# Key products made once and kept masked in DRAM, and a new order of the feature tiles in a two-layer streaming trunk

## The chip, the cores and the metric

The kernel runs on one core of one Trainium2 chip. The metric is device time in microseconds (us) of one execution; the median of the runs is compared. One more execution was taken with the hardware profiler, and all views below are of that one.

## The reference

Two layers are applied to 1024 prompt tokens and to 8 samples of 16 tokens, which share the weights. Each layer projects the normed input once and feeds four branches; the change touches the first, a recurrent mix with a matrix state for each of 4 heads:

```python
z = rms_norm(x, p['norm_g']) @ p['w_in']
...
prev = jnp.concatenate([shift_prev[:, None, :], za[:, :-1]], axis=1)
zs = za + p['rw_mu'] * (prev - za)          # receptance r, key k, value v, two low-rank inputs
...
def step(s, inp):
    r_t, w_t, k_t, v_t, kk_t, a_t = inp
    sa = jnp.einsum('bhij,bhj->bhi', s, -kk_t)
    s = (s * w_t[:, :, None, :] + sa[:, :, :, None] * (kk_t * a_t)[:, :, None, :]
         + v_t[:, :, :, None] * k_t[:, :, None, :])
    return s, jnp.einsum('bhij,bhj->bhi', s, r_t)
...
s_t, ys = lax.scan(step, s0, xs)
y = layer_norm(ys) ; out = y + sum(r * k * rk) * v
...
out = x + (concat(A, B, C, D) * silu(gates)) @ p['w_out']
```

The other branches are latent attention, a gated unit over 128 positions, and a pooling of trailing means.

## The kernel before

All 1152 tokens are columns, in three groups g of G = 384. The input projection is done by feature tiles of 128 rows: 24 in each layer, in the order F_ORDER (line 35), each as 3 groups of 24 matmuls of 128x384 into a PSUM tile `pj` (two buffers), because operands and weights are split into a high and a low part. `project` (line 245) runs a list of tiles. `load_weights` (line 229) fetches a tile's weights in four pieces on SP's queue, two tiles ahead; ACT makes the high part `wh`, POOL the low part `wl`. After each group a sink reads `pj`: for keys, receptances and values it is `shift_sink` (line 376), ACT and DVE together.

All other work is written as Python generators in lanes. At the matmul numbers in `ticks`, and at the end of each group, `tick()` advances each lane by one step; `inproj` (line 360) sets how many ticks a tile has (two, three or four in a group: 6, 9 or 12 in a tile). Lane "a" carries the recurrent branch, in this order: `a_elem` (line 427) makes the key operands `KB` and `AR` of one group; `systems` (line 506) makes for each 64-token chunk (16 of the prompt, then 16 and 17 of the samples) four products of keys with keys, masks them on DVE into `ns`, and ACT's queue stores them in `nd` or `nds` in DRAM; after 4 idle steps `solve` (line 520) loads the diagonal blocks and inverts them row by row with two DVE operations for each row: 15 rows for the samples (32 partitions), then 31 rows for the prompt (128 partitions), and stores the results in `dd` and `dds`. `recurrence` (line 707) then takes the chunks one after another, the samples first, three steps each: `prepare` (line 560) of the next chunk loads the solved blocks `tt` and makes `Gm`, the masked products of keys with keys and receptances, again with PE and DVE; `advance` (line 639) moves the state. `groupnorm` (line 722) follows for each group in lane "n".

The order of feature tiles is WDAD and K0 together, K1, R0, R1, V0, V1, D0, GD0, D1, GD1, VC0, VC1, U0, GC0, U1, GC1 (lines 910 to 929), then seven more for attention and gates. `systems` starts in K1, `solve` in V0; `recurrence` is queued after D0, so that its 56 steps run in GD0 to U0. Instructions are put on their engines by a scheduler that follows the written order as a priority but may issue an instruction earlier when its inputs are ready; each engine then works in that order. `Gm`, `tt` and `ns` have two buffers each, the tag "m" for large tiles has eight, PSUM tiles `b` four.

## Time and profile before

| | us |
|---|---|
| median of 3 runs | 1447.55 (1444.83 to 1448.42) |
| the profiled execution | 1447.32, of it a span of 1445.5 |
| PE busy | 1358.6 |
| DVE, ACT, POOL busy | 786.8, 746.6, 465.2 |
| tiles K1 to GC1, first layer | 326.17, of it PE busy 305.41 |
| tiles K1 to GC1, second layer | 319.88, of it PE busy 302.88 |

PE = TensorE's matmuls, PEld its weight loads, DVE = VectorE, ACT = ScalarE, POOL = GpSimd, SP = SyncE, which issues loads. A q behind an engine's name marks its sequencer: an issue of a transfer or a wait. Busy is the time in which an engine has at least one instruction in work; a wait is listed with the instruction that ended it.

### The profile page before, as it was taken

The page shows a single profiled execution, that of the slowest core. Times are in us where ns is not written, and L with a number is a line of the kernel's source. Part 1 is how long each engine was busy: PE and PEld are TensorE (multiplying, and loading weights), DVE is VectorE, ACT ScalarE, POOL GpSimd, SP SyncE. Part 2 cuts the span into 40 slices and gives each one's busy share as a digit, 9 for nine tenths or more (in the row PEclk, how much of TensorE's full clock was granted, in tenths as well). Part 3 has the DMA queues.
Part 4 walks back from the last instruction along what each step waited for, and adds up shares of the span by engine and source line. Part 5 has one row for each costly group of instructions (what it writes and reads, how often), then busy time and mean ns, then how long its engine had stood idle before and what let it go on. Part 6 is the DMA issues. An engine that isn't in the chain of part 4 may idle for free. (4 is left out here: it accounts for less than half of the span.)

```text
span 1445.5 us, 26910 instructions
## 1 busy us (share of the span) xinstructions
PE 1358.6 (94%) x9962; PEld 1160.2 (80%) x9962; DVE 786.8 (54%) x1766; ACT 746.6 (52%) x2013; POOL 465.2 (32%) x600
## 2 busy tenths in 40 slices
PE   4899989999999999999989998999999999899999
PEld 3768868888988886679977788788789788766998
DVE  6984954435235567742287948444532374777211
ACT  6762234655466677642257621555654676866210
POOL 4514404336411033332162234232653111322320
PEclk9799999999999999999999999999999999999999
DMA  7113241110312214033300122321022111131232
GB/s 222 52 32 75 63 102 42 61 49 25 96 46 70 60 37 128 5 116 93 99 22 30 49 64 66 92 69 49 29 71 74 52 57 59 45 103 45 74 95 77
DMA packets 116596, 97.40 MB, mean 67 GB/s; under 512 B 46129, under 2 KB 111345, under 8 KB 116465
## 3 DMA queue, kind: packets, MB, share of 16 engines
q1 hardware_dynamic: 76776, 73.74, 17.6%
q10 hardware_dynamic: 39688, 21.94, 5.1%
q8 instruction: 79, 1.29, 0.4%
q14 instruction: 53, 0.43, 0.1%
HBM read 71.48 MB, written 24.16 MB: 66 GB/s over the span
## 5 line engine op out<-in xcount | busy, mean ns | idle before, releaser
L76 PE MATMUL pj<-xh,wh 128*128 128x384 f32 x1152 | 415.4, 361 | 18.9 <-ACT xh L280 7.2
L76 PE MATMUL pj<-xl,wh 128*128 128x384 f32 x1152 | 396.4, 344 | 2.4 <-POOL xl L282 2.0
L76 PE MATMUL pj<-xh,wl 128*128 128x384 f32 x1152 | 396.3, 344 | 0.0
L242 POOL TENSOR_TENSOR wl<-wr,wh 128x256 fp32r<-128x256 f32 x200 | 157.0, 793 | 465.9 <-ACT wh L241 390.5
L76 PEld LDWEIGHTS pj<-xh,wh 128*128 128x128 f32 x1152 | 221.6, 193 | 41.7 <-ACT sho L400 11.3
L76 PEld LDWEIGHTS pj<-xl,wh 128*128 128x128 f32 x1152 | 222.1, 193 | 9.0 <-POOL xl L282 3.3
L76 PEld LDWEIGHTS pj<-xh,wl 128*128 128x128 f32 x1152 | 221.4, 192 | 6.0 <-issue 4.8
L76 PE MATMUL pj<-yh,wh 128*128 128x384 f32 x384 | 129.3, 337 | 2.4 <-DVE x L1426 2.4
L76 PE MATMUL pj<-yh,wl 128*128 128x384 f32 x384 | 128.6, 335 | 0.0
L76 PE MATMUL pj<-yl,wh 128*128 128x384 f32 x384 | 128.3, 334 | 0.0
L241 ACT ACTIVATE wh<-wr 128x256 fp32r<-128x256 f32 x200 | 81.0, 414 | 84.7 <-PE pj L76 41.0
L242 POOL TENSOR_TENSOR wl<-m,wh 128x256 fp32r<-128x256 f32 x56 | 43.7, 790 | 102.0 <-ACT wh L241 84.4
L76 PEld LDWEIGHTS pj<-yh,wh 128*128 128x128 f32 x384 | 72.1, 188 | 3.7 <-DVE x L1426 2.8
L76 PEld LDWEIGHTS pj<-yl,wh 128*128 128x128 f32 x384 | 72.1, 188 | 0.1
L76 PEld LDWEIGHTS pj<-yh,wl 128*128 128x128 f32 x384 | 72.1, 188 | 0.1
L1293 ACT ACTIVATE X<-b,ng 128x512 f32<-128x512 f32 (+3 forms) x96 | 55.0, 577 | 25.3 <-DVE ng L1285 21.4
L76 PE MATMUL b<-sp,cr 128*128 128x384 f32 (+3 forms) x192 | 59.5, 385 | 3.2 <-POOL sp L99 2.8
L1281 DVE TENSOR_REDUCE mx<-b 128x1 f32<-128x512 f32 (+3 forms) x96 | 53.0, 556 | 9.8 <-PE b L76 8.0
L1422 DVE TENSOR_TENSOR pt<-pj,pt 128x384 f32<-128x384 f32 x24 | 13.4, 557 | 80.6 <-PE pj L76 80.6
L76 PEld LDWEIGHTS st<-X,X 128*64 128x64 f32 x576 | 35.1, 136 | 27.4 <-ACT X L1311 7.6
L241 ACT ACTIVATE wh<-m 128x256 fp32r<-128x256 f32 x56 | 22.4, 413 | 61.0 <-PE pj L76 59.9
L1304 PE MATMUL pj<-cm,X 128*128 128x128 f32 x288 | 48.0, 286 | 5.0 <-ACT X L1293 5.0
(307 smaller groups left out, 2591.7 us busy)
## 6 DMA issues: line engine op xcount, KB each, us to landing
wr<-in_win_dram SPq DMA_DIRECT2D x176, 128.0 KB
m<-in_wout_dram SPq DMA_DIRECT2D x12, 512.0 KB
x<-in_xT_dram SPq DMA_DIRECT2D x12, 384.0 KB
ysp<-m ACTq DMA_DIRECT2D x24, 192.0 KB
pt<-in_xT_dram SPq DMA_DIRECT2D x24, 192.0 KB
ea<-ysp SPq DMA_DIRECT2D x24, 192.0 KB
x1d<-x ACTq DMA_DIRECT2D x24, 192.0 KB
pt<-x1d SPq DMA_DIRECT2D x24, 192.0 KB
```

The lines of the kernel that those rows point to most:

```text
L76: return PE.matmul(out, lhsT=lhsT, rhs=rhs, start=start, stop=stop, skip_group_check=True)
L241: A.activation(out=h, in_=r, func=AF.Copy)
L242: Po.tensor_tensor(out=lo, in0=r, in1=h.bitcast(F32), op=ALU.subtract)
L1281: V.tensor_reduce(out=mx[:, b:b + 1], in_=pc[:, :w], axis=AX.X, op=ALU.max)
L1293: A.activation(out=P[:, :w], in_=pc[:, :w], func=AF.Exp, scale=SCALE, bias=ng, accum_out=sums[pr][:, b, s, h:h + 1])
L1304: PE.transpose(ptp[:, j * 128:(j + 1) * 128], Pb[slot][:, j * 128:(j + 1) * 128], ident)
L1422: V.tensor_tensor(out=xr, in0=ps, in1=xr, op=ALU.add)
```

## The change

- `systems` makes the full products of `Gm` for each chunk (keys with keys and receptances, two groups of PE products and two masks on DVE), stores the two halves of the key part in `nd` or `nds`, and stores the whole of `Gm` in a new DRAM tile `gd`; all three on SP's queue. The separate 64x64 products and `ns` are gone. It takes one step for each chunk instead of one for two.
- `prepare` loads `Gm` from `gd` instead of making it.
- Because `Gm` needs the receptances, `systems(g)` is queued by the sink of R1. The tile order becomes WDAD and K0, V0, R0, K1, R1, V1, D0, GD0, D1, and so on. `solve` follows directly; the idle steps are gone.
- `recurrence` is queued after D1 instead of D0; the tiles from GD1 to GC1 have 12 ticks each (U0 had them before, the others 9).
- The 30 operations of the sample solve go to POOL, issued in one step, with their own scratch `TMs`; the prompt's stay on DVE.

```diff
@@ -32,7 +32,7 @@
 (WDAD, K0, R0, V0, K1, R1, V1, D0, GD0, D1, GD1, VC0, VC1, U0, GC0, U1, GC1,
  GB0, GB1, Q0, Q1K, CK, GA0, GA1) = range(NF)
 
-F_ORDER = (WDAD, K0, K1, R0, R1, V0, V1, D0, GD0, D1, GD1, VC0, VC1, U0, GC0, U1, GC1,
+F_ORDER = (WDAD, K0, V0, R0, K1, R1, V1, D0, GD0, D1, GD1, VC0, VC1, U0, GC0, U1, GC1,
            Q0, Q1K, CK, GB0, GB1, GA0, GA1)
 
 
@@ -359,10 +359,9 @@
 
         def inproj(f, sink):
             ticks = (3,)
-            if f in (K1, R0, R1, V0, V1, D0, GD0, D1, GD1, VC0, VC1, GC0, U1, GC1,
-                     GA0, GA1):
+            if f in (K1, R0, R1, V0, V1, D0, GD0, D1, GA0, GA1):
                 ticks = (2, 5)
-            elif f in (U0, GB0, GB1):
+            elif f in (GD1, VC0, VC1, U0, GC0, U1, GC1, GB0, GB1):
                 ticks = (1, 3, 5)
             project([(l, f)], xh, xl, [sink], ticks)
 
@@ -490,6 +489,8 @@
             def after(g, zs):
                 ex = AR[i][g][:, :, 1, :]
                 Po.tensor_tensor(out=ex, in0=chv(zs), in1=ex, op=ALU.mult)
+                if i == 1:
+                    go("a", systems(g))
             shifted(fr, lambda g: s_tile("gn", 3), after)
 
         def values(fv):
@@ -498,7 +499,9 @@
             vfm.append(v)
 
 
+
         nd, nds = halves(f"nd{l}", 32, 64), halves(f"nds{l}", 4, 64)
+        gd = dr.tile([18, 128, 512], F32, tag=f"gd{l}", name=nm("gd"))
 
         def hp(h):
             return slice(64 * (h % 2), 64 * (h % 2) + 64)
@@ -506,46 +509,53 @@
         def systems(g):
             for cl in range(6):
                 c = 6 * g + cl
-                pn = pb()[:, 0:128].rearrange("p (i t) -> p i t", i=2)
-                for h in range(4):
-                    mm(pn[hp(h), h // 2, :], KB[h // 2][g][hp(h), cl, h % 2, :], AR[h // 2][g][hp(h), cl, 0, :])
-                ns = chp.tile([128, 2, 64], F32, tag="u0", name=nm("ns"), bufs=2)
-                mk = cm[:, C_MP if c < 16 else C_MS, 0:64]
-                V.tensor_tensor(out=ns, in0=pn, in1=mk.unsqueeze(1).broadcast_to([128, 2, 64]), op=ALU.mult)
-                A.dma_start(out=whole(nd, c, 64) if c < 16 else whole(nds, c - 16, 64),
-                            in_=ns.rearrange("p i t -> p (i t)"))
-                if cl % 2:
-                    yield
+                samp = c >= 16
+                Gm = chp.tile([128, 2, 2, 128], F32, tag="gm", name=nm("gm"), bufs=2)
+                mk = cm[:, C_MS if samp else C_MP, :]
+                for hh in range(2):
+                    pg = pb()[:, 0:256].rearrange("p (i t) -> p i t", i=2)
+                    pr = slice(64 * hh, 64 * hh + 64)
+                    for i in range(2):
+                        mm(pg[:, i, :], KB[i][g][pr, cl].rearrange("p a t -> p (a t)"),
+                           AR[i][g][pr, cl].rearrange("p a t -> p (a t)"))
+                    V.tensor_tensor(out=Gm[:, hh], in0=pg, in1=mk.unsqueeze(1).broadcast_to([128, 2, 128]),
+                                    op=ALU.mult)
+                for hh in range(2):
+                    half = nds[2 * (c - 16) + hh] if samp else nd[2 * c + hh]
+                    SY.dma_start(out=half[0:128 * 64].rearrange("(s i t) -> s i t", s=64, i=2),
+                                 in_=Gm[64 * hh:64 * hh + 64, hh, :, 0:64])
+                SY.dma_start(out=gd[c], in_=Gm.rearrange("p h i t -> p (h i t)"))
+                yield
 
         def solve():
             NT = m_tile(1024).rearrange("p (s t) -> p s t", s=32)
             DT = m_tile(1024).rearrange("p (s t) -> p s t", s=32)
-            sol = m_tile(768)
-            TM = sol[:, 0:256]
+            sol = m_tile(832)
+            TM, TMs = sol[:, 0:256], sol[:, 768:832]
             NTs = sol[:, 256:512].rearrange("p (s t) -> p s t", s=16)
             DTs = sol[:, 512:768].rearrange("p (s t) -> p s t", s=16)
             for i in range(2):
                 SY.dma_start(out=NT[64 * i:64 * i + 64], in_=diagonal(nd, i, 32, 64))
                 SY.dma_start(out=NTs[16 * i:16 * i + 16], in_=diagonal(nds, i, 16, 64))
 
-            def invert(NTt, DTt, n, np_):
+            def invert(E, TM, NTt, DTt, n, np_):
                 full = DTt[0:np_]
                 Po.memset(full, 0.0)
                 Po.memset(full.rearrange("p s t -> p (s t)")[:, 0:n * n:n + 1], 1.0)
                 for s in range(n - 1):
                     w = n - 1 - s
                     tm = TM[0:np_, 0:(s + 1) * w].rearrange("p (j t) -> p j t", t=w)
-                    V.tensor_tensor(out=tm, in0=full[:, 0:s + 1, s:s + 1].broadcast_to([np_, s + 1, w]),
+                    E.tensor_tensor(out=tm, in0=full[:, 0:s + 1, s:s + 1].broadcast_to([np_, s + 1, w]),
                                     in1=NTt[0:np_, s:s + 1, s + 1:n].broadcast_to([np_, s + 1, w]), op=ALU.mult)
-                    V.tensor_tensor(out=full[:, 0:s + 1, s + 1:n], in0=full[:, 0:s + 1, s + 1:n], in1=tm, op=ALU.add)
+                    E.tensor_tensor(out=full[:, 0:s + 1, s + 1:n], in0=full[:, 0:s + 1, s + 1:n], in1=tm, op=ALU.add)
                     if s % 3 == 2:
                         yield
 
-            yield from invert(NTs, DTs, 16, 32)
+            for _ in invert(Po, TMs, NTs, DTs, 16, 32):
+                pass
             for i in range(2):
                 A.dma_start(out=diagonal(dds, i, 16, 64), in_=DTs[16 * i:16 * i + 16])
-            yield
-            yield from invert(NT, DT, 32, 128)
+            yield from invert(V, TM, NT, DT, 32, 128)
             DN = NT
             V.tensor_copy(out=DN, in_=DT.rearrange("p s t -> p t s"))
             for i in range(2):
@@ -571,15 +581,7 @@
                 SY.dma_start(out=tt.rearrange("p i t -> p (i t)"), in_=whole(dd, c, 128))
 
             Gm = chp.tile([128, 2, 2, 128], F32, tag="gm", name=nm("gm"), bufs=2)
-            for hh in range(2):
-                pg = pb()[:, 0:256].rearrange("p (i t) -> p i t", i=2)
-                pr = slice(64 * hh, 64 * hh + 64)
-                for i in range(2):
-                    mm(pg[:, i, :], KB[i][g][pr, cl].rearrange("p a t -> p (a t)"),
-                       AR[i][g][pr, cl].rearrange("p a t -> p (a t)"))
-                V.tensor_tensor(out=Gm[:, hh], in0=pg,
-                                in1=cm[:, C_MS if samp else C_MP, :].unsqueeze(1).broadcast_to([128, 2, 128]),
-                                op=ALU.mult)
+            SY.dma_start(out=Gm.rearrange("p h i t -> p (h i t)"), in_=gd[c])
 
             pt = pb()
             for i in range(2):
@@ -904,26 +906,21 @@
 
         def after_k1(g, zs):
             start("a", a_elem(1, g, zs))
-            if g > 0:
-                go("a", systems(g - 1))
 
         project([(l, WDAD), (l, K0)], xh, xl,
                 [shift_sink(WDAD, lambda g: z6[:, gcols(g)], tanh_part),
                  shift_sink(K0, lambda g: zk0[:, gcols(g)], lambda g, zs: start("a", a_elem(0, g, zs)))])
+        values(V0)
+        receptance(0, R0)
         shifted(K1, lambda g: zk1[:, gcols(g)], after_k1)
-        go("a", idle(4))
-        go("a", systems(2))
-        go("a", idle(4))
+        receptance(1, R1)
         go("a", solve())
-        receptance(0, R0)
-        receptance(1, R1)
-        values(V0)
         values(V1)
         A.dma_start(out=shift_o[l], in_=sho)
         pool_in(0, D0)
-        go("a", recurrence())
         pool_gate(0, GD0)
         pool_in(1, D1)
+        go("a", recurrence())
         pool_gate(1, GD1)
         gating()
         finish("a")
```

## Rows read from the trace of the kernel before

**Rows 1.** The page of the kernel before: its first line, and its part 1 (busy time of each engine, share of the span, number of instructions).
```profile
span 1445.5 us, 26910 instructions
...
PE 1358.6 (94%) x9962; PEld 1160.2 (80%) x9962; DVE 786.8 (54%) x1766; ACT 746.6 (52%) x2013; POOL 465.2 (32%) x600
```
**Rows 2.** Table of stretches. Columns: the stretch from:to in us and its length; busy us of PE, PEld, DVE, ACT and POOL with the number of instructions; mean granted TensorE clock (1.00 is the level of 2.4 GHz); busy share of the DMA engines; GB/s. The stretches are feature tiles of the second layer in this order: R1, D0, GD0, VC1, U0, U1; the last two are all tiles from K1 to GC1, in the first layer and in the second.
```profile
825.29:843.03 17.74, 15.98 (x130) 14.32 (x129) 8.76 (x21) 3.48 (x10) 6.72 (x8) 1.00 0.20 61
...
871.33:885.27 13.94, 12.75 (x74) 12.43 (x73) 13.36 (x28) 3.37 (x9) 6.93 (x11) 1.00 0.23 69
885.27:922.08 36.81, 31.27 (x312) 26.61 (x311) 25.05 (x56) 12.62 (x41) 8.80 (x13) 0.91 0.38 80
...
998.03:1022.44 24.41, 24.41 (x305) 21.15 (x303) 6.75 (x19) 11.40 (x43) 4.51 (x6) 1.00 0.21 64
1022.44:1055.15 32.71, 29.66 (x349) 24.77 (x349) 20.40 (x53) 19.98 (x73) 22.22 (x28) 1.00 0.09 26
...
1073.69:1086.41 12.72, 12.72 (x75) 12.59 (x73) 1.74 (x4) 4.58 (x11) 6.54 (x10) 1.00 0.50 154
...
68.46:394.63 326.17, 305.41 (x2767) 265.76 (x2767) 177.35 (x408) 150.61 (x455) 123.52 (x161) 0.98 0.22 60
781.98:1101.86 319.88, 302.88 (x2770) 263.83 (x2769) 177.24 (x405) 151.90 (x459) 123.40 (x161) 0.99 0.22 61
```
**Rows 3.** Waits of PE in the tiles K1 to GC1 of the second layer, the longest in total first (who waited for whom: us in total, times, longest us).
```profile
PE b L76 <- DVE gm L580: 2.9, 1, 2.9
PE pj L76 <- ACT sho L400: 1.9, 2, 1.1
...
PE b L76 <- DVE ns L514: 1.8, 2, 0.9
...
PE b L76 <- DVE S L677: 1.2, 2, 0.9
```
**Rows 4.** The same for the tiles K1 to GC1 of the first layer.
```profile
PE b L76 <- DVE gm L580: 3.2, 2, 3.0
PE b L76 <- DVE S L677: 2.8, 2, 1.9
PE b L76 <- DVE ns L514: 1.9, 2, 1.0
PE pj L76 <- ACT sho L400: 1.8, 2, 1.1
...
PE b L76 <- DMA tt<-dd: 1.6, 1, 1.6
```
**Rows 5.** Groups of instructions over the whole execution, different shapes apart: line, engine, operation, tiles, shapes, number | busy us, mean ns of one | idle time of the engine before them and what ended it. PE's first row is the products for `Gm`, its second those for `ns` (a 32-bit matmul leaves two records); DVE's rows are the masking of each.
```profile
L580 DVE TENSOR_TENSOR gm<-b,cm 128x256 f32<-128x256 f32 x72 | 28.3, 418 | 6.2 <-PE b L76 6.1
L76 PE MATMUL b<-ar,kb 64*128 64x128 f32 x288 | 27.9, 298 | 0.0
...
L76 PE MATMUL b<-ar,kb 64*64 64x64 f32 x288 | 15.3, 228 | 4.6 <-DVE ns L514 3.7 <-DVE kb L481 0.8
...
L514 DVE TENSOR_TENSOR ns<-b,cm 128x128 f32<-128x128 f32 x36 | 10.4, 288 | 22.5 <-DMA nd<-ns 21.1 <-PE pj L76 1.3
```
**Rows 6.** The same view for the tile R1 of the second layer alone.
```profile
L76 PE MATMUL b<-ar,kb 64*64 64x64 f32 x56 | 2.7, 227 | 1.8 <-DVE ns L514 1.8
```
**Rows 7.** The chain that ended last, in order of time, in the second layer from the key products to the results of the solve: start us, us, what.
```profile
828.34 4.41 DMA nd<-ns
833.20 3.06 DMA nd<-ns
...
898.75 1.09 DVE m L550
...
900.72 2.58 ACTq L552
```
**Rows 8.** Timelines of DVE, ACT, POOL, SP and PE in the first layer, put in order of time (start us, us, engine, line, operation, tiles, shapes): an early instruction of the head norm on DVE; ACT's store of the last `ns`; the first operations of the sample solve on DVE and one of POOL beside them; the first multiply of the prompt solve; SP's first load of `tt` and PE's first product with it; a load of `tt` in steady recurrence.
```profile
133.59 1.30 DVE L728 SCALAR_TENSOR_TENSOR gn<-ar,vcs,kb 64x384 f32<-64x384 f32 x2
...
133.70 0.50 ACTq L515 DMA_DIRECT2D nds<-ns  x1
...
143.11 0.16 DVE L538 TENSOR_TENSOR m<-m 32x15 f32<-32x15 f32 x1 [0.86 <-POOL wl L242]
...
143.29 0.74 POOL L242 TENSOR_TENSOR wl<-wr,wh 128x256 fp32r<-128x256 f32 x1 [0.30 <-ACT wh L241]
...
143.31 0.75 DVE L540 TENSOR_TENSOR m<-m 32x15 f32<-32x15 f32 x1
144.09 0.17 DVE L538 TENSOR_TENSOR m<-m 32x28 f32<-32x28 f32 x1
...
151.94 0.19 DVE L538 TENSOR_TENSOR m<-m,m 128x31 f32<-128x31 f32 x1
...
197.03 0.50 SPq L571 DMA_DIRECT2D tt<-dd  x1
...
204.06 0.37 PE L76 MATMUL b<-tt,gm 64*64 64x32 f32 x8
...
220.33 0.51 SPq L571 DMA_DIRECT2D tt<-dd  x1
```
**Rows 9.** All executions of one of POOL's small operations with two inputs (number, then min/median/max ns, first and last start, shapes).
```profile
L797 POOL TENSOR_TENSOR m<-pf,m x8: 214/244/393, 169.4 to 934.4; 64x16 f32<-64x16 f32 x8
```
**Rows 10.** The DMA view of the stretch 221 to 226 us, which holds the packets of the last load of Rows 8 alone: queue, kind: packets, MB, share of the time of 16 engines.
```profile
q1 hardware_dynamic: 130, 0.13, 8.9%
```

## The prediction

> **What bounds the kernel now.** I read in this order: the page's first two lines, a table of stretches by feature tile, PE's waits inside these tiles, the groups of instructions by shape, and the chain of work. PE is busy 1358.6 of 1445.5 us [rows 1]; no other engine is over 54%. One tile without company costs PE 12.72 us, all of them busy (U1), and VC1, with three chunks of the recurrence beside it, has 24.41 us and no idle [rows 2]. So a us of work taken off PE is a us off the time wherever PE has no wait, and the place to look for the rest is its waits. From K1 to GC1, all that the change touches, PE idles 326.17 - 305.41 = 20.8 us in the first layer and 319.88 - 302.88 = 17.0 us in the second [rows 2], 37.8 us in all. The largest single waits are those for the masking of Gm in GD0, where DVE still works on the solve: 2.9 and 3.2 us [rows 3, 4]. GD0 alone idles 36.81 - 31.27 = 5.5 us, and its mean granted clock is 0.91 (between the two levels) [rows 2]. The chain shows the same place from the other side: from the stores of ns over the solve (L538 to L550) to the stores of dd it runs through DVE and DMA, not PE [rows 7]. PE's work is the bound, and this latency chain is what it runs into.
>
> **The sum is made against the profiled execution**, 1447.3 us (1445.5 of span and 1.8 around it), which stands 0.2 us under the median of the runs.
>
> **1. Products made once.** The 4 products for ns of each chunk go, both layers: 288 records, 15.3 us of PE [rows 5]. A second reading: in R1 56 of them (7 chunks) are busy 2.7 us [rows 6], so 36 chunks give 13.9. I take -15. Those for Gm (27.9 us) and their masking (28.3 us of DVE) are moved, not saved [rows 5]; the masking of ns (10.4 us) goes, beside other work, at nothing. What each chunk now issues while the systems are made: two PE groups, two masks of 418 ns, and three SP transfers (two halves, gd) where ACT issued one.
>
> **2. The wait for a Gm buffer.** There are two, and each is held until its three stores have landed. Today DVE waits 21.1 us for ns in the same way [rows 5], and PE gets 1.8 and 1.9 us of it [rows 3, 4]. After: PE makes a chunk per tick, a tile with 9 ticks takes 12.7 + 9 x 27.9/36 = 19.7 us, so two chunks 4.4 us. A buffer's turn is 2 x 0.42 for the masks, about 1.0 for the first two issues (0.5 each, as for tt [rows 8]) and the landing of gd. By the stores of ns, 3.06 to 4.41 us [rows 7], the turn is 4.9 to 6.2 us and the wait 0.25 to 0.9 us a chunk: 9 to 33 us over 36 chunks; if gd lands in under 2.5 us it is 0. The PE runs two chunks ahead in its own PSUM buffers, which hides the first of it. I take 4, what goes with ns (3.7), so 0 net; ends -4 and +29. Behind the waiting mask on DVE lie the shift sums that free pj, behind the waiting store on SP the weight pieces; PE waits for both.
>
> One row bears on which end is nearer. A load of tt (128 KB, leading dimension 2) keeps 8.9% of 16 engines busy for 5 us [rows 10], 7.1 us of one engine's work; a landing after 3.6 us of it means two engines. The Trainium skill, page "DMA: Bandwidth & Descriptors", section "Why a DMA increments its semaphore by 16 and not by 1", says that a transfer is spread over the largest number up to 16 that divides its slowest dimension on both sides; the row agrees. By it the halves (64 rows) and gd (128 rows) use all 16, gd would land in about 2 us, an estimate, and this term would be -4 instead of 0.
>
> **3. The solve and the start of the recurrence.** Gm no longer queues behind the solve on DVE: -6.1 (2.9 + 3.2). What is late next is dd. In the first layer the last ns is stored at 133.70 and the sample solve begins at 143.11, 9.4 us later; from the first prompt multiply at 151.94 to the first load of tt at 197.03 are 45.1 us; PE uses it at 204.06 [rows 8]. After, counted from the start of D0: the last key products are in its second tick, 5.5 us; masks 0.8; the same 9.4; the prompt solve begins at 15.7, the load of tt is issued at 60.8, and lands at 66, since one load has 3.6 us of packets after 1.3 us of issue. PE gets there after D0 (13.9 as now, waits for the busy DVE included [rows 2], and 1.6 of key products), GD0 (the same 13.9 and about 2 for its gate products), D1 (13.9) and part of GD1: from the start of GD0 at 173.3 to 204.06 PE needs 30.7 us now, less 5.5 of waits [rows 2], less 2.3 for the Gm of three chunks, less 2.5 because seven ticks of twelve come after fewer of the tile's own products than seven of nine: 20. That is 65. So PE waits some 1 us in each layer if the solve runs as now. Behind this wait on PE stand the tile's own products. The sample solve on Pool is 30 operations, each between 0.21 and 0.39 us [rows 9], 6 to 12 us; ahead of it on Pool is nothing, behind it are the weight pieces of D1 (needed 12 us later) and D0's windows, which cover it just so. On DVE it frees 143.11 to 151.94, 8.8 us, off the chain already counted. I take 4 us a layer, nearer to the 1 of the chain than to the 12.5 of the Pool rival, because some of Pool's operations will fall beside DVE's: 8 in all, +2 net; ends -6 (nothing is late) and +19 (12.5 a layer).
>
> **4. Denser ticks, later.** The recurrence's 56 steps go from 9 ticks a tile to 12, GD1 to GC0, and still end before U1. U0 has 12 ticks already: there PE waits 1.2 us for the state (L677) [rows 3]. 56 steps are 4.7 such tiles: 5.6 us a layer, 11 in all, against 2.8 + 1.2 = 4.0 now [rows 3, 4]; but DVE no longer masks Gm there, 0.84 us of a chunk's 6.2. I take +3; ends -4 and +7.
>
> **5. Loading Gm.** Each chunk's load stands behind tt's on SP and waits for the buffer of two chunks back. tt has one wait today, 1.6 us [rows 4], at 8 us a chunk (24.41 / 3 [rows 2]). At 12 ticks a tick carries 1.0 us of it (24.41 - 12.7 in VC1, less 2.3 for Gm, over 9), and the chunk takes (12.7 + 12 x 1.0) / 4 = 6.2 us: some 5 us for tt and 1 for Gm fit with little left. I take +2; ends -2 and +32 (1 us each of 32 prompt chunks).
>
> **6. Values and receptances first.** They lie between K0 and K1, so the key elements of K0 have two tiles to finish. The waits for sho (1.9 and 1.8 [rows 3, 4]) may halve: -2; ends -4 and 0. ACT loses 36 issues of 0.5 us [rows 8], at nothing, as it is 52% busy [rows 1].
>
> **Sum:** -15 + 0 + 2 + 3 + 2 - 2 = -10, so 1437 us; the likeliest case's own range is 1429 to 1443.
>
> **Rivals.** *The waits go as well.* For it: DVE loses ns and the sample solve, and VC1 shows that PE can run without idle. Against: GD0. Then -15 - 3.7 - 6.1 = -25: 1422 us (range 1416 to 1429).
>
> *The loads take the gain back.* If each of 32 prompt chunks waits 0.3 us for tt or Gm, 8 more than term 5 has: 1445 us (1443 to 1452), no measurable change. For it: the 6.2 us above. Against: one wait of 32 now.
>
> *Pool's solve holds up DVE's* (slower). For it: an operation of the sample solve takes 0.75 us while Pool subtracts beside it, its neighbours without Pool 0.16 and 0.17 [rows 8]; it began 0.02 us after Pool's and ended as that was over. If every one of Pool's 30 operations delays DVE's solve by its length, 6 to 12 us, the upper end puts dd 11.5 us later: 12.5 us a layer in place of 4, +17 on the sum: 1454 us (1452 to 1460). It decides from a wait of about 11 us a layer. Against: only half of the 62 prompt operations run beside it, and instructions are issued in an order found ahead, with projections in the holes. The Trainium skill, page "SBUF — State Buffer", section "SBUF: two separate sides", calls the pair of ports that DVE and GpSimd share an exclusive lock, held for a whole instruction when DVE reads two SBUF inputs; the trace agrees. By that rule the move to Pool gains nothing, and this rival's 1454 us follows instead of 1437.
>
> *It doesn't do what it says.* The order in the text is not the order issued: a head norm written behind the recurrence runs at 133.59, before the solve [rows 8]. If recurrence and solve are issued where they were, terms 3 to 5 shrink and term 1 stays: 1435 to 1443.
>
> **How the numbers follow.** Chances: forecast 0.42, waits go 0.20, loads 0.15, Pool 0.18, order 0.05. A measurement of this kernel can tell about 0.3%, 4.3 us, from no change. Faster by more (under 1443.2): 0.42 + 0.20 + 0.05, less 0.03 at the forecast's edge, 0.64. Within: 0.15 + 0.03 = 0.18. Slower: 0.18. The range leaves out half of the best case (under 1421) and half of the slower one (over 1454): 1421 to 1454; the far ends of terms 2 and 5 lie beyond it.
>
> **What would show it.** Right: no 64x64 products of keys; 288 records of 64x128 now in R1 to D0; under 2 us a layer of PE waiting for masks there; no wait for gm L580's successor in GD1. Term 3: a wait of PE for tt or dd in GD1, 2 to 6 us; over 8, with solve operations of DVE over 0.6 us, is the Pool rival. Terms 4 and 5: PE's waits for S and for Gm or tt in GD1 to GC0, 5 us a layer. What would make it wrong: idle in K1 to GC1 well off the 38 us that I keep almost whole.

## The result and the profile after

The changed kernel took 1467.01 us (median of 4 runs, 1465.80 to 1467.44), the kernel before 1447.72 us beside it (4 runs): ratio 1.0136, 95% interval 1.0118 to 1.0153. It is slower by 19.3 us, where 1437 us were forecast with a range of 1421 to 1454. The profiled execution took 1447.32 us before and 1467.44 us after.

The page of the changed kernel, first line and busy times:
```profile
span 1465.4 us, 26502 instructions
...
PE 1361.8 (93%) x9674; PEld 1159.8 (79%) x9674; DVE 776.6 (53%) x1670; ACT 743.5 (51%) x2013; POOL 482.7 (33%) x660
```
PE has 288 records less than in [rows 1], those of the 64x64 key products, and is busy 3.2 us more.

The table of stretches of the changed kernel (columns as in [rows 2]). The first eight stretches are tiles of the second layer: R1, V1, D0, GD0, D1, GD1, VC1, U0. Then follow the stretch from the start of D0 to PE's first product with a prompt chunk's `tt`, and all tiles from V0 to GC1 in the first and in the second layer.
```profile
834.85:855.61 20.76, 18.85 (x108) 15.63 (x108) 20.39 (x39) 11.68 (x30) 5.72 (x9) 1.00 0.16 50
855.61:878.84 23.23, 22.50 (x153) 18.64 (x153) 10.31 (x28) 3.67 (x11) 5.00 (x7) 1.00 0.49 158
...
878.84:896.16 17.32, 16.73 (x106) 15.10 (x105) 9.65 (x20) 3.36 (x9) 7.49 (x13) 1.00 0.62 172
896.16:916.23 20.07, 14.64 (x80) 13.49 (x79) 11.87 (x31) 4.89 (x12) 14.45 (x41) 0.99 0.52 87
916.23:930.18 13.95, 13.95 (x72) 13.95 (x73) 13.44 (x24) 4.39 (x10) 8.55 (x13) 0.89 0.37 113
930.18:973.08 42.90, 32.18 (x295) 26.18 (x294) 24.34 (x46) 12.43 (x42) 14.08 (x19) 0.80 0.46 101
...
1001.76:1031.29 29.53, 28.18 (x360) 23.84 (x357) 12.59 (x25) 19.33 (x66) 11.35 (x13) 1.00 0.29 87
1031.29:1062.06 30.77, 29.39 (x371) 24.49 (x369) 14.77 (x43) 19.30 (x77) 19.11 (x26) 1.00 0.27 86
...
878.84:963.92 85.08, 68.33 (x469) 61.95 (x469) 57.92 (x117) 22.27 (x60) 43.85 (x82) 0.92 0.48 107
...
68.09:401.21 333.12, 305.41 (x2623) 264.87 (x2622) 172.34 (x360) 149.03 (x455) 131.90 (x191) 0.97 0.31 87
788.77:1121.33 332.56, 306.18 (x2626) 264.66 (x2625) 172.07 (x357) 150.22 (x459) 132.09 (x191) 0.97 0.31 87
```
Against the last two of [rows 2] the tiles take 7.0 and 12.7 us more, 19.6 together: all of the loss. PE is idle there 27.7 and 26.4 us, where it was 20.8 and 17.0: 16.3 us more; the other 3.3 are busy time. So there are two sums to explain: busy +3.3 where -15 was forecast, and idle +16.3 where +5 was.

The idle has one place. In the kernel before the same stretch of the second layer is
```profile
871.33:915.87 44.54, 38.05 (x312) 34.14 (x313) 34.74 (x75) 11.53 (x35) 14.13 (x21) 0.92 0.36 78
```
with 44.54 - 38.05 = 6.5 us of idle. After, it is 85.08 - 68.33 = 16.75 us. In the first layer (159.26 to 204.06 before, 159.81 to 245.41 after) it is 7.7 and 17.75. That is 20.3 us more in both layers; everywhere else in these tiles the idle fell by 3.9.

Who waits in it, by PE's waits from GD0 to VC0 of the second layer (us in total, times, longest):
```profile
PE pj L76 <- DVE pt L761: 6.8, 2, 5.4
PE b L76 <- ACT m L612: 6.0, 1, 6.0
PE b L76 <- DMA gm<-gd: 2.7, 2, 1.9
PE b L76 <- ACT vu L597: 1.5, 1, 1.5
```
The first row is the silu of GD0 that frees `pj`, the second the copy of `YS` for the sample chunks. None of them is a wait for `dd`, but the stretch ends with it: the first load of `tt` is issued at 956.15 and PE uses it at 963.92.

**Why the silu is late** is read on ACT's timeline:
```profile
905.88 0.62 ACT L759 ACTIVATE pt<-pt,eps 128x384 f32<-128x384 f32 x1
914.17 0.84 ACTq L557 DMA_DIRECT2D dds<-m  x2
915.06 0.52 ACT L760 ACTIVATE pt<-pt 128x384 f32<-128x384 f32 x1 [8.56 <-POOL m L550]
```
ACT stands at the store of the sample inverses until Pool has finished that solve (913.91 + 0.22), and the silu's last step stands behind the store.

**Why the solve is late** is read on SP's timeline; D0 begins at 878.84:
```profile
881.15 0.58 SPq L527 DMA_DIRECT2D gd<-gm  x1
881.83 0.39 SPq L238 DMA_DIRECT2D wr<-in_win_dram  x1
882.31 1.17 SPq L525 DMA_DIRECT2D nd<-gm  x2
883.53 0.58 SPq L527 DMA_DIRECT2D gd<-gm  x1
884.29 1.17 SPq L525 DMA_DIRECT2D nd<-gm  x2
...
890.54 0.58 SPq L527 DMA_DIRECT2D gd<-gm  x1
```
A chunk costs SP about 1.9 us of issues, 2.4 with a weight piece, and they stand nearly back to back; DVE waits 12.0 us for stores of `gd` before it may write the next `Gm`. The prompt solve's multiplies on DVE in the same layer:
```profile
L548 DVE TENSOR_TENSOR m<-m,m x31: 192/401/952, 901.3 to 945.6; 128x31 f32<-128x31 f32 x2, 128x60 f32<-128x60 f32 x2, 128x87 f32<-128x87 f32 x2, 128x112 f32<-128x112 f32 x2
```
It begins 22.4 us behind the start of D0, and lasts 44.7 us with the additions. Before, in that layer, it went from 864.00 to 898.72: it began 7.3 us ahead of D0 and lasted 34.7.

The last thing that it waited for was not a store but Pool:
```profile
901.10 0.16 POOL L544 MEMSET m<- 128x32 f32 x1
901.29 0.19 DVE L548 TENSOR_TENSOR m<-m,m 128x31 f32<-128x31 f32 x1 [0.74 <-POOL m L544]
```
This memset writes the diagonal of the unit matrix that the solve starts from, and on Pool it stood behind D0's windows (the running sums of the pooling branch, made by Pool and DVE). The second load of `nd` was issued at 894.93; in systems_m below, where the memset was done 12 us ahead of the solve, such a load ended the wait 4.4 us behind its issue. By that it was in at about 899.3 here (an estimate), so some 2 of the 22.4 us come from D0's windows and the memset behind them, and the rest from the stores and loads.

### The profile page after: what moved, and what is told of

It is laid out like the page before. It is cut to its first block, busy times and chain, and to the rows that moved or that the text cites. A ratio compares the mean times of both kernels' runs of the same rounds, so it can differ in the third digit from the quotient of the medians.

```text
span 1465.4 us, 26502 instructions
## 1 busy us (share of the span) xinstructions
PE 1361.8 (93%) x9674; PEld 1159.8 (79%) x9674; DVE 776.6 (53%) x1670; ACT 743.5 (51%) x2013; POOL 482.7 (33%) x660
## 5 line engine op out<-in xcount | busy, mean ns | idle before, releaser
L76 PEld LDWEIGHTS pj<-xh,wh 128*128 128x128 f32 x1152 | 222.3, 193 | 49.1 <-DVE pt L761 17.1
```

The costliest lines, as they stand in the source:

```text
L76: return PE.matmul(out, lhsT=lhsT, rhs=rhs, start=start, stop=stop, skip_group_check=True)
```

## The experiments

Ratios are to the kernel before on the same chip; the changed kernel's is 1.0136. "Idle" is PE's from the start of D0 to the first use of a prompt chunk's `tt`, in the second layer (6.5 before, 16.7 changed).

### Waits taken away one at a time

**dds_sp**: `A.dma_start(out=diagonal(dds, ...` becomes `SY.dma_start(...`.

> The changed kernel with one edit: the two stores of the sample inverses (L557) are issued by SP and not by ACT; all PE instructions stay in the same order. Queue theory: ACT stood at these stores until Pool had finished the sample solve, and the silu of GD0 (L758 to L761) stood behind them, so PE waited 6.56 and 5.43 us at the first product of D1. Then those two waits fall under 1 us each. Of the 12.0 us part comes back as a wait for YS or dd in GD1, since the solve on DVE ends no earlier: 1455 to 1462 us. Port theory (Pool's operations hold up DVE's, and DVE is late with the silu): the waits stay over 4 us a layer, 1465 to 1468 us.

1464.87 us, 1.0119 (1.0104 to 1.0134). GD0's wait is gone (GD0 14.18 us), but D1 now holds one of 6.2 us for the same silu line, and the idle is still 16.7. SP stood at the store, a weight piece behind it was issued only at 913.47, and ACT had nothing to do from 908.83 to 916.20, when that piece was in, with a silu behind it. The queue theory is right for the wait and wrong for the time.

**ys_own**: `ysm = m_tile(512)` becomes two tiles `s_tile("gn", 3, 256)`.

> The changed kernel with one edit: the products of the sample states, YS (written at L612), lie in two tiles of the ring gn and not in a tile of the ring m. Slot theory: since the recurrence was queued behind D1, YS takes the slot that D1's own tile leaves, so ACT's copy waits for the last window of D1 (943.80) and PE for the copy, 5.44 and 5.96 us. Then these waits fall under 1 us, and the copy runs as soon as its product is there. The prompt chunks still wait for dd, so not all of the 11.4 us is gained: 1456 to 1463 us. Rival (dd sets the pace of GD1 whatever YS does): the time stays, 1465 to 1468 us, and the wait moves to tt.

1464.50 us, 1.0123 (1.0107 to 1.0139). The copy no longer waits for D1's window, and PE waits 7.4 us for it all the same: ACT now stands at the stores of `dd` ahead of it, until DVE ends the prompt solve at 944.54. The slot held it up, but was not the limit.

**dds_ys**: both edits.

> The changed kernel with both edits: the sample inverses stored by SP, YS in tiles of its own. Queue and slot theory: 23.4 us of PE's waits in D1 and GD1 are touched, and dd is the next late thing; 1444 to 1456 us, with D1 and GD1 at a higher granted clock than 0.86 and 0.80. Port theory, or dd as the pace: 1460 to 1467 us.

1461.70 us, 1.0096 (1.0081 to 1.0111): 6 us below the changed kernel by the ratios, idle 14.2.

**pin**, **pin_ys**: the sample inverses are stored by ACT behind GD0's last silu, `dd` by SP; pin_ys also has YS in its own tiles. The edit in short:
```diff
+ while St.get("n", 0) < 3: yield
+ behind(St["silu"], lambda: A.dma_start(out=diagonal(dds, ...
- A.dma_start(out=diagonal(dd, ...      (two forms)
+ SY.dma_start(out=diagonal(dd, ...
```


> The changed kernel with the stores of the solve out of ACT's way: the sample inverses are stored by ACT behind GD0's last silu, and dd by SP. Queue theory: the waits of 6.56 and 5.43 us at D1's first product fall under 1.5 us; DVE's solve is no longer stopped for 4.9 us by the silu's multiply that waits for ACT, so dd lands some 5 us sooner; the wait for YS (L612) stays, as D1's windows do: 1448 to 1458 us. Rival (the weight pieces, whose low half Pool makes behind the sample solve, are the next late thing, as they were when SP stored the sample inverses): a wait of 4 us or more a layer in D1, 1458 to 1465 us.

> As pin, and YS in tiles of its own (as in ys_own). With no store of the solve ahead of it on ACT, the copy of YS runs as soon as its product is there, and PE waits in GD1 only for dd: 1442 to 1452 us, no wait for the copy of YS over 1 us. If the wait passes to tt and dd whole, the time of pin, 1450 to 1458 us.

1467.45 us, 1.0130 (1.0106 to 1.0155), and 1465.91 us, 1.0132 (1.0113 to 1.0151). Idle 17.1 and 15.4. PE's waits from GD0 to VC0 in pin_ys:
```profile
PE b L76 <- DVE u L658: 7.4, 1, 7.4
PE pj L76 <- DVE pt L763: 4.0, 1, 4.0
PE b L76 <- issue: 3.9, 1, 3.9
```
No wait for YS; now the sample chunk's addition on DVE stands behind the end of the solve (940.43), and then the prompt chunk waits for `tt`. Both expectations fell: in five kernels the wait that was aimed at went or changed its place, and 13.5 to 17.1 us of idle stayed.

### Parts alone, or left out

**dve**: `invert(Po, ...)` becomes `invert(V, ...)` for the samples.

> The changed kernel with the sample solve on DVE again, in the same place of the program; the rest as it is. If Pool is what made the change slow (its queue, or its operations beside DVE's), PE's wait of 6.56 and 5.43 us at the first product of D1 goes, and the prompt solve, 44.7 us in the changed kernel against 34.9 before, is short again: 1452 to 1460 us. Late solve theory: the sample systems land at 902.4 only, so DVE begins both solves after that and ends the prompt one no sooner than Pool's version; the store of the sample inverses then comes 2 to 4 us sooner, and dd at about the same time: 1462 to 1470 us.

1464.73 us, 1.0131 (1.0108 to 1.0153), no different from the changed kernel. Idle 13.7. Pool's solve alone is not what made the change slow.

**pool_only**: the kernel before with `solve` of the changed kernel.

> The kernel before with one part of the change: the sample solve on Pool, in one piece, and the prompt solve on DVE from the start; order, products and recurrence as before. If Pool's solve costs by itself (port, or ACT's queue behind the store of the sample inverses), 1450 to 1458 us, with waits of PE for sinks in V0 to D0. If it helps, as the solve ends some 5 us sooner and GD0 waits 5.5 and 6.7 us today: 1438 to 1446 us.

1449.49 us, 1.0017 (1.0005 to 1.0030). PE waits 7.9 us in V1 for a sink behind ACT's store of the sample inverses, and idles 2.7 us in place of 6.5 from D0 on: one wait for another.

**later_only**: the kernel before with `recurrence()` queued behind D1 and the changed ticks.

> The kernel before with one part of the change: the recurrence is queued behind D1, and GD1 to GC1 have twelve ticks each. dd is there before the recurrence asks for it, so the waits for masks in GD0 go. If the late start is good by itself: 1435 to 1441 us. If YS, which takes a slot that D1's windows leave late, holds up ACT and PE even so, and the denser steps wait for the state: 1446 to 1456 us, with a wait for L610's successor of ACT of 4 us a layer or more in GD1.

1459.98 us, 1.0090 (1.0072 to 1.0108). The late start costs some 13 us by itself, though the solve ends as early as before (27.0 us behind the start of D0). Stretch from D0 to the first use of `tt`, then D1:
```profile
877.32:951.09 73.77, 60.90 (x439) 56.68 (x440) 43.55 (x87) 18.87 (x51) 32.12 (x47) 0.91 0.29 65
917.99:930.79 12.80, 12.80 (x74) 12.67 (x73) 3.26 (x4) 3.85 (x9) 7.59 (x12) 1.00 0.27 83
```
12.9 us of idle. PE waits 9.0 us at the end of GD0 for its silu, which stands on ACT behind D0's last windows and then the stores of `dd`. Before, PE had the sample chunks to do beside that. What was expected to hold it up (YS) did not.

**later_sp**, **before_sp**: the four stores of `dd` on SP, in later_only and in the kernel before.

> The kernel before with the later recurrence and its twelve ticks (as in later_only), and the four stores of dd issued by SP and not by ACT. Queue theory: in later_only ACT stands at these stores from 900.54 to 910.3 with GD0's silu behind them, and PE waits 9.0 and 9.4 us for it at D1's first product at a granted clock of 0.81; with the stores on SP this wait falls under 2 us a layer, and the time comes down from 1460 to 1436 to 1446 us. Rival (the late start costs by its dense steps, or DVE's solve itself holds up the silu's multiply): the wait stays over 5 us, 1453 to 1460 us.

> The kernel before with the four stores of dd issued by SP and not by ACT; nothing else. ACT stands there from 890.58 to 904.87 too, but PE has the sample chunks to do in GD0. If the stores on ACT are what GD0 waits for, its idle 5.5 and 6.7 us go in part: 1438 to 1444 us. If the masks of Gm behind the solve on DVE are, as the trace puts it down, or SP's weights now stand behind the stores: 1445 to 1450 us.

1456.45 us, 1.0064 (1.0047 to 1.0080), and 1449.88 us, 1.0027 (1.0016 to 1.0039). In later_sp the wait falls from 9.0 to 4.8 us, and 3.3 and 1.6 us for masks of `Gm` appear in GD1. ACT's queue is under a third of what the late start costs; in the kernel before the stores are better left on ACT.

**twice**: the changed kernel with `systems` and the making of `Gm` in `prepare` as before.

> The changed kernel without the products made once: systems makes the 64x64 key products again (two chunks a tick, stored by ACT, as before), the recurrence makes its own Gm and masks it, and nothing is kept in DRAM; order, later start, ticks and the solve on Pool stay. If the products made once are worth the 15 us that the prediction gave them, this kernel takes 1482 us. If the separate groups of products between projections (about 0.9 us a chunk, 36 chunks, for 0.66 in a group that is there anyway) and the waits for the Gm buffers and loads take it back, it takes 1463 to 1471 us. The key part V0 to D0 then takes some 100 us a layer in place of 109 and 107.4, and GD1 to GC1 is longer by the masks.

1462.79 us, 1.0110 (1.0093 to 1.0126): the changed kernel is not faster for making the products once. Its solve begins 11.3 us behind the start of D0 and its idle is 16.0, so this is not the products alone; the groups themselves are counted further down. From later_only it differs by the order of the tiles, the sample solve on Pool and the idle steps; 1.0110 and 1.0090 have intervals that overlap, so most of its loss can be that of the late start.

**early**: the changed kernel with the recurrence and its ticks as before.

> The changed kernel with the recurrence queued behind D0 and the ticks of GD1 to GC1 as before; products once, their buffers and the solve as changed, so the solve begins 20 to 22 us after the start of D0. Late solve theory: the recurrence asks for dd after 36 to 38 us of PE's work from D0's start and gets it after 80 to 90 us; PE is idle 40 to 50 us a layer there, 1505 to 1535 us. Then the later start was what kept the late solve from costing this. Rival (PE's waits come from queues and slots behind the late start): 1450 to 1470 us.

1487.59 us, 1.0278 (1.0257 to 1.0299). With the late solve, the late start is worth 20 us. The idle is 21.1 us, not 40 to 50:
```profile
893.61:977.72 84.11, 63.00 (x440) 56.59 (x439) 52.42 (x113) 19.28 (x54) 41.54 (x80) 0.88 0.44 105
```
63.0 us of PE's work stand ahead of the first use of `tt`, where the expectation had 38: the order of PE's instructions is another, with the projections ahead. So the idle is not simply the end of the solve less a fixed amount of PE's work.

### The solve sooner

**pairs**: a `yield` after every second chunk of `systems`.

> The changed kernel with one edit: systems makes two chunks in a tick (a yield after every second chunk), so 9 groups of key products lie between the projections instead of 18. Late solve theory: the solve starts too late, because the key products reach into D0's third group; it then starts some 9 us sooner (the masks still wait for a Gm buffer, 2.3 us a chunk), and most of the 16 to 17 us that PE waits a layer in GD0 to GD1 goes, less 3 to 6 us of PE waiting for masks in R1 and V1: 1445 to 1456 us. Burst theory (what was lost is the entry and exit of each group of products): 18 groups less by 0.2 us, 4 to 7 us in both layers: 1460 to 1463 us, with the waits in GD1 as they are.

1472.38 us, 1.0180 (1.0162 to 1.0198). The solve begins 20.1 us behind D0, only 2.3 sooner; idle 18.7. Neither theory foresaw a loss.

**systems_m**: pairs, and `G2 = m_tile(1024)` for each pair in place of two `gm` tiles.

> The changed kernel with the key products in pairs, two chunks a tick, and each pair's Gm in a tile of the ring m in place of the two gm tiles, so that no mask waits for a store: the solve can begin where it did before, 7 us ahead of D0, in place of 22.4 us behind its start. Late solve theory (PE's waits in GD0 to VC0 are one debt, the time at which dd can be used, 85.1 us after D0's start, less the 68 us of work that PE has until then, and taking a store out of the way only moves it): the debt of 16.7 us goes whole; but as in later_only GD0's silu still waits behind D0's windows and the solve with no recurrence beside it, so 9 to 13 us of idle stay between D0 and the first use of tt: 1451 to 1459 us. If the late start of the recurrence is harmless by itself: 1435 to 1446 us. If the solve's place doesn't matter: 1463 to 1469 us.

1467.47 us, 1.0144 (1.0123 to 1.0164). The solve begins at 14.1, not at -7. DVE's last mask ends at 875.23, yet SP's timeline shows:
```profile
885.37 1.16 SPq L527 DMA_DIRECT2D nd<-m  x2
886.58 0.59 SPq L529 DMA_DIRECT2D gd<-m  x1
887.26 1.17 SPq L527 DMA_DIRECT2D nds<-m  x2
888.49 0.58 SPq L529 DMA_DIRECT2D gd<-m  x1
889.17 1.18 SPq L527 DMA_DIRECT2D nds<-m  x2
890.39 0.59 SPq L529 DMA_DIRECT2D gd<-m  x1
891.07 0.61 SPq L541 DMA_DIRECT2D m<-nd  x1
```
With buffers to spare, SP is still issuing stores 15.7 us later, 1.9 us a chunk without a hole: 18 chunks are 34 us. Here the issues are the pace.

**early_m**, **early_m_pool**: systems_m with the recurrence and ticks as before; the samples on DVE, or on Pool.

> Products made once and order as changed; key products in pairs with Gm in tiles of the ring m; the recurrence and its ticks as before, behind D0; the sample solve on DVE as before. So of the change only the products made once and the order of the tiles stay, with the solve no later than before. Late solve and cover theory: the recurrence's groups are cheaper by the products of Gm (74.4 us net a layer against 82.6 measured), nine groups of key products cost 2 to 3 us a layer more than before, GD0's waits for masks (2.9 and 3.2 us) go: 1430 to 1442 us. If products made once bring nothing even so (the loads of Gm wait, the groups between the projections cost as much): 1445 to 1455 us.

> As early_m, with the sample solve on Pool. As in pool_only, ACT's store of the sample inverses stops the sinks in V1 or D0 for up to 8 us a layer and the solve ends some 5 us sooner with less idle in GD0: within 4 us of early_m, 1430 to 1446 us. If Pool's operations beside DVE's cost more: 1447 to 1455 us.

1474.18 us, 1.0191 (1.0164 to 1.0218), and 1487.84 us, 1.0282 (1.0262 to 1.0301). Idle 16.7 and 20.7. With samples on Pool the solve ends 55.1 us behind the start of D0, on DVE 49.3: here Pool's solve does cost, about 13 us by the ratios.

**gd_act**, **early_split**: in the changed kernel `gd` stored by ACT; and early_m with the issues shared.
```diff
- SY.dma_start(out=half...                        (early_split)
+ (SY, A)[hh].dma_start(out=half...
+ if cl % 2: SY.dma_start(out=gd[c - 1:c + 1]...   once a pair
```


> The changed kernel with one edit: the stores of gd are issued by ACT, the halves still by SP. Issue theory: SP's issues pace the key products (three transfers of 0.5 to 0.6 us a chunk stood back to back on SP in systems_m, some 1.9 us a chunk, while its masks were long done, and so the solve began 14 us after D0's start though the last key products came in V1). With one issue less the waits of DVE for a Gm buffer shorten, the solve begins 5 to 7 us sooner than 22.4 us after D0's start, as the prediction had it (15.7), and the idle of 16.7 us a layer between D0 and the first use of tt falls to 9 to 13: 1453 to 1461 us. Buffer theory (the landing of gd is the pace, whoever issues it): the solve begins at 21 to 23 us, 1465 to 1469 us.

> As early_m (products once, in pairs, Gm in the ring m, recurrence and ticks and DVE's solve as before), with the issues shared out: of each chunk one half by SP and one by ACT, gd once a pair by SP, so SP has 16 us of them a layer in place of 31 to 34. Issue theory: the solve, which began 14.3 us after D0's start in early_m, begins 0 to 8 us ahead of it, as before the change; GD0 and D1 lose their waits of 4.8 and 11.9 us: 1434 to 1446 us, below early_m's 1474 by 28 us or more. Rival (the queue isn't the cause, the solve is late for another reason, such as the landing of the last stores or Pool's windows ahead of the memsets): the solve begins after D0's start by 8 us or more, 1460 to 1475 us.

gd_act: 1472.84 us, 1.0173 (1.0156 to 1.0191); the solve begins at 20.8 in place of 22.4, idle 19.6, and the edit made it slower. Here neither a load nor the memset (done at 896.99) ended the wait: DVE worked at D0's windows until 903.98, 0.03 us ahead of the solve. So in the changed kernel SP's issues are not alone in holding the pace. early_split: 1473.27 us, 1.0177 (1.0160 to 1.0195): the solve begins 2.1 us behind D0 in place of 14.3, which is what the issue theory says, and the time does not move. The stretch to the first use of `tt` in early_split:
```profile
879.19:941.40 62.21, 47.25 (x353) 43.12 (x352) 45.52 (x124) 17.21 (x49) 20.61 (x29) 0.92 0.41 94
```
15.0 us of idle, 7.8 of it for the copy of YS. The solve lasts 44.3 us there, as the sample solve and D0's windows lie among its operations. PE is busy 1358.4 us on the whole page, as before (1358.6): all 22 us that this profiled execution has more are idle, 16 of them in this stretch of the two layers.

No version beat the kernel before.

## Why the prediction was wrong, point by point

**Term 1, -15 for products made once: the step that failed first.** The 288 records are gone, as forecast. But "moved, not saved" was taken to mean that the moved products of `Gm` cost the same in their new place, and a group of small products has another price alone than in company. PE's timeline of the changed kernel shows a group of `Gm`'s products alone between projections, and a group of the recurrence without them:
```profile
874.78 0.34 PE L76 MATMUL pj<-xh,wl 128*128 128x384 f32 x1
875.05 0.72 PE L76 MATMUL b<-ar,kb 64*128 64x128 f32 x8
875.70 0.45 PE L76 MATMUL pj<-xh,wh 128*128 128x384 f32 x1
...
987.96 0.34 PE L76 MATMUL pj<-xh,wl 128*128 128x384 f32 x1
988.23 0.45 PE L76 MATMUL b<-S,ar 64*64 64x64 f32 x8
988.61 0.44 PE L588 MATMUL b<-cm,kb 128*128 128x128 f32 x2
988.88 0.38 PE L590 MATMUL b<-cm,m 128*64 128x128 f32 x2
989.02 0.42 PE L76 MATMUL pj<-xh,wh 128*128 128x384 f32 x1
```
and that of twice the same group of the recurrence with them:
```profile
970.13 0.34 PE L76 MATMUL pj<-xh,wl 128*128 128x384 f32 x1
970.40 0.45 PE L76 MATMUL b<-S,ar 64*64 64x64 f32 x8
970.78 0.72 PE L76 MATMUL b<-ar,kb 64*128 64x128 f32 x8
971.43 0.44 PE L589 MATMUL b<-cm,kb 128*128 128x128 f32 x2
971.71 0.38 PE L591 MATMUL b<-cm,m 128*64 128x128 f32 x2
971.84 0.42 PE L76 MATMUL pj<-xh,wh 128*128 128x384 f32 x1
```
From projection to projection: alone 875.70 - 874.78 = 0.92, less the 0.17 that a projection step takes anyway, 0.75 us a chunk. In company (971.84 - 970.13) - (989.02 - 987.96) = 0.65. Summed so over every group of the second layer, without the idle: key products 9.3 us before and 17.2 after, recurrence with the group norm's products 82.0 and 74.4; in the first layer 10.7 and 17.0, 82.6 and 73.1. So the key part gained 14.2 us and the recurrence lost 17.1: the term is worth about -3, not -15 (-5 if the group norm's own groups, 8 a layer in place of 4, are left out).

Put by chunk: the old key products took 20.0 us with them, more than the 15 of the forecast. The new groups cost 34.2, 0.95 a chunk: 0.75 is the cheapest, and those that PE reaches after a wait cost up to 1.14 without the wait. In the recurrence only 17.1 came free, 0.48 a chunk; 36 times 0.65 would be 23.4, and what took the other 6 is not parted. PE's busy time agrees: on the pages of the fourteen kernels with products made once it is 1354.4 to 1372.0 us, against 1358.6 before, and none shows 15 us less. The range had no end for this term but -13.9 to -15; one from the row of the same group alone was missing.

**Term 2, no net wait for a `Gm` buffer: right for PE, blind for the solve.** PE waits 1.8 and 1.5 us for masks, 3.3 where 4 was taken. The landing was nearer to the shorter of the two values weighed, about 2 us: of the `gd` store issued at 883.53 DVE had its buffer back at 885.95. What was not asked is who else waits: DVE waits 12.0 us for stores of `gd`, and the last halves leave 15 us behind the start of D0.

**Term 3, +2 for the start of the recurrence: the largest miss.** Forecast: solve begins 15.7 us behind the start of D0, `tt` asked for at 60.8, used at 66, PE's need 65. Measured: 22.4, 77.3, 85.1, and PE's work 68.3. The need was about right (its 5.5 us of waits in GD0 are the second layer's; the first layer, from which the rest is taken, has 36.93 - 30.25 = 6.7). The chain is 19 us longer: 6.7 by the late begin of the solve (the last store, and some 2 us of D0's windows and the memset), 9.8 by a solve of 44.7 us in place of 34.9, and 2.6 between the load of `tt` and its use. Of these 9.8, 4.9 are a ring of waits (DVE stood from 910.70 to 915.61 at GD0's silu, which waited for ACT, which waited for Pool); its own operations took 30.9 us in place of 26.5. Idle in this stretch rose by 20.3, against +2 net. The forecast counted a wait for `dd` alone; the runs showed waits for the silu and for YS in its place, behind the solve in the queues of ACT and DVE.

**Terms 4 and 5, +3 and +2.** Waits for S nearly vanish (1.0 us in the first layer), those for `gm` are 3.6 and 2.7 us; those for the split of an operand into its high and low part (L99 on Pool) rose from 0.3 to 1.8 us in each layer. With the rest they are a little better than forecast: the idle outside the stretch fell by 3.9.

**Term 6, -2: right.** The wait for `sho` went from 1.8 and 1.9 us to 0.4 and 0.4.

Summed: busy 18 us worse (12 by term 1; of the rest PE at a lower clock is seen in D1, 13.95 us at 0.89, in later_only 12.80 at 1.00; some 5 us are not placed), idle in the stretch 18 worse, other idle 7 better: 29 of the 30 us between 1437 and 1467.

**The rival of Pool and DVE** came nearest in time (1454) but not for its reason. Of its mark the operations over 0.6 us are there, but none of PE's waits of over 2 us is for `tt` or `dd`, and dve, with the samples on DVE, is as slow. During the sample solve DVE's operations stay near their length; the long ones fall beside Pool's weight pieces and windows, as before the change. That its 1454 lies nearer to 1467 than the forecast does is luck.

**Shown and not shown.** Shown: the loss is idle between D0 and the first prompt chunk, plus a term 1 of -3; the parts do not add up (the late start costs 13 us alone and saves 20 with the late solve). Shown too that none of the waits taken away is the limit by itself: in the fourteen kernels with products made once, the changed one among them, the idle stays between 13.5 and 21.1 us in the second layer, whether the solve begins 2 or 22 us behind D0. Open is what sets that remainder. Nearly every edit also gave the engines' queues another order, and solve, windows, silu and sample chunks cross in those of DVE, ACT and SP at once, so the runs do not part them. Not tried: the order of the tiles alone in the kernel before, and the memset of the solve ahead of D0's windows on Pool.

## What to carry to other kernels

Price a moved group of small matmuls from projection to projection in its new place, alone and in company; the busy time of its instructions (27.9 us for 36 chunks, 0.78 each) told neither the 0.95 paid nor the 0.48 freed. When results that were consumed in place are stored instead, sum the issues on the queue that stores them and ask when the last one leaves, before costing who reads them. And where an in-order queue holds a store that waits for a long solve, moving the store moves the wait; look for the end of the chain, and for the work that covered it before.

## What the runs showed of the hardware that was not expected

Issuing counts: three stores a chunk of 0.5 to 0.6 us each, with one weight piece among them, kept SP busy nearly without a hole for 37 us (854.04 to 890.98 in systems_m), at transfers of 32 and 256 KB alike.

The same operation of the solve on DVE takes 0.42 us where Pool has nothing in work, and twice that beside Pool's weight piece (919.50 to 920.24):
```profile
919.63 0.89 DVE L548 TENSOR_TENSOR m<-m,m 128x255 f32<-128x255 f32 x1
...
922.68 0.42 DVE L548 TENSOR_TENSOR m<-m,m 128x255 f32<-128x255 f32 x1
```
Beside the 30 small operations of the sample solve on Pool (211 to 365 ns each) its instructions took 0.25 to 0.41 us, but for one of 0.98 that fell on a weight piece (905.28 to 906.00). The Trainium skill, page "SBUF — State Buffer", section "SBUF: two separate sides", has the pair of ports of DVE and GpSimd as an exclusive lock held for a whole instruction. The pair of rows agrees; beside the small operations no such hold is seen. What the rule would make of the sample solve, no gain from the move to Pool, is what dve measured in the changed kernel (1.0131 against 1.0136), but these rows do not give the lock as the reason.

The mean granted clock was 0.89 in D1, right behind the wait of 5.4 us, and 0.80 in GD1, which holds that of 6.0, between the levels of 1.2 and 2.4 GHz. In later_only, where the wait of 9.0 us ends 6.5 us ahead of D1, GD0 had 0.81 and D1 1.00.
